# Attention's row maxima from the high parts alone: two heads as a pair of matmuls on the upper and lower 64 rows of TensorE's array

## The chip, the cores and the metric

The kernel runs on one core of a Trainium2 chip. A core has a matrix engine (TensorE, in the profile PE for its matmuls and PEld for its weight loads), three engines for everything else (VectorE is DVE, ScalarE is ACT, GpSimd is POOL), and SyncE (SP), which here issues most of the DMA transfers. The metric is the time of one execution on the device, in microseconds (us); lower is better.

## The reference

One layer of an encoder: RMSNorm, one input projection, grouped-query attention beside a Hyena operator (long convolutions through Fourier transforms), an output projection, an MLP, a last RMSNorm. The change touches the attention, of 2048 positions, 8 query heads and 2 key/value heads of 64 elements:

```python
def one_block(q_blk):
    s = jnp.einsum('bqkgd,bskd->bkgqs', q_blk, k, preferred_element_type=jnp.float32) * scale
    p = jax.nn.softmax(s, axis=-1).astype(v.dtype)
    return jnp.einsum('bkgqs,bskd->bqkgd', p, v)

o = lax.map(one_block, qb)          # blocks of 128 queries
```

The softmax subtracts a bound from the scores of each query before the exponential. Any number near the row's maximum does, since it cancels in the quotient; the kernel works out such a bound from the scores themselves.

## The kernel before, in words

**Precision.** Where float32 accuracy is wanted, a number is split into a high part that TensorE's fast format (`F32R`) holds exactly, and the low rest. `mm3` makes one product of three matmuls of such parts (its lines L158, L159, L160 are shared by the whole kernel). In the attention, a query column of 128 rows in `q` holds the 64 high parts of a head in its upper half (rows 0 to 63) and the 64 low parts in its lower half. A key tile `kt` comes in two versions: the first repeats the high parts of the keys in both halves of the rows, so one matmul of 128 rows gives (high + low of q) times (high of k).

**Units.** `attention` goes through 32 units: a unit is one block of 128 queries (`NT` = 16 blocks) for the four heads (`G`) that share a key/value head (`NKV` = 2). Each unit is 16 steps of `peak` and 16 steps of `weights`, and `peak` runs `AHEAD` = 22 steps earlier.

- `peak(u, i)`: for one head and one of four blocks of 512 keys, one 128x128 by 128x512 matmul into a PSUM bank `sc` (L454), and one VectorE reduction to the maximum of each query (`top`, L457). There are three `sc` banks; the tiles `sh` and `of` take theirs from the same three. After step 15, VectorE forms `low` and `diag` of the 16 maxima of a query.
- `shift`: one matmul (`sh`, L467) turns the maxima into the lower rows of `q2`, so that the score matmul subtracts them.
- `weights(u, j)`: for one block of 128 keys and all four heads, two matmuls into a bank `st` (L474, L475), ScalarE's exponential into `p` (L477, `PB` buffers), and GpSimd's running sum (L482).
- `weighted`: eight steps' products `p` times the values (`o`, L495), in plain float32. Even and odd key blocks use a weight tile of 64 columns each, in the left and the right half of the array's columns (the profile writes 128*64); their outputs are the upper and lower halves of one bank.
- `finish`: four small matmuls (`of`, L506), the division, and the store.

**Side work.** Each step also pumps one piece of other work, `side`: the taps of the long filter (`ft`, L1200) and the projection `uo` (`u_proj`, through `mm3`), whose weights VectorE splits (`uw`, L356).

**Order.** In this part of the program the order of each engine's instructions is set by a scheduler, which starts from the order of the calls above and moves instructions by what is ready. The parts that come later are written down in a fixed order. `load_q` is called by `begin` one unit ahead; `q` and `q2` have three buffers each, and their loads stand in SP's queue.

Of the kernel before, what the change touches and what calls it, by code (L numbers as in the profile page):

```python
# [12 lines left out]
F32R = mybir.dt.float32r  # L13
I32 = mybir.dt.int32
AF = mybir.ActivationFunctionType
ALU = mybir.AluOpType
AX = mybir.AxisListType
# [3 lines left out]
P = 128  # L21
# [4 lines left out]
HD = 64  # L26
NQ = 8
NKV = 2
G = NQ // NKV
# [8 lines left out]
def f32(ap):  # L38
    return ap.bitcast(F32)
# [126 lines left out]
def qkv_proj(k, pa, ps, side):  # L166
# [126 lines left out]
    for i in range(-1 - XL, NT + FL):  # L293
        if i == 13:
            k.first = load_q(k, 0), {(0, b): load_k(k, k.early, 0, b, 4) for b in range(2)}, load_v(k, k.early, 0)
        if 1 < i + XL + 2 < NT:
            xt[i + XL + 2] = load_x(i + XL + 2)
        e = i - FL
        ending = 0 <= e < NT
        if ending:  # L300
            finish(e, *hl[e], 0)
        if 1 < i < NT:
            oq[i] = project(*aT[i], 0, QW)
        if ending:
            finish(e, *hl[e], 1)
        if 0 <= i + 1 < NT:
            aT[i + 1] = turned(i + 1, xs.pop(i + 1))
        if 0 <= i + XL + 1 < NT:
            xs[i + XL + 1] = normed(i + XL + 1, xt.pop(i + XL + 1))
        if 0 <= i + 1 < 2:  # L310
            oq[i + 1] = project(*aT[i + 1], 0, QW)
        pump(side, 1 if i > 0 else 0)
        if ending:
            finish(e, *hl.pop(e), 2)
        if 0 <= i < NT:
            okv = project(*aT.pop(i), QW, 256)
        if 0 <= i - 1 < NT:
            hl[i - 1] = twice(norm_rope(i - 1, *yz.pop(i - 1)))
        if 0 <= i < NT:
            yz[i] = taken(i, oq.pop(i), okv)  # L320
# [89 lines left out]
def load_k(k, pool, kv, b, bufs):  # L410

    c = []
    for part in range(2):
        t = pool.tile([P, 512], F32R, name="kt", bufs=bufs)
        k.nc.sync.dma_start(out=f32(t[:]), in_=k.k_d[kv, part, :, b * 512:(b + 1) * 512])
        c.append(t)
    return c


def load_q(k, n):  # L420

    kv, t = n // NT, n % NT
    q = k.early.tile([P, G, P], F32R, name="q", bufs=3)
    q2 = k.early.tile([P, G, P], F32R, name="q2", bufs=3)
    src = k.q_d[kv * G:(kv + 1) * G, :, t * P:(t + 1) * P].rearrange("h p t -> p h t")
    k.nc.sync.dma_start(out=f32(q[:]), in_=src)
    k.nc.sync.dma_start(out=f32(q2[:HD]), in_=src[:HD])
    return q, q2


def load_v(k, pool, half):
    v = pool.tile([P, NT // 2, NKV, HD], F32, name="vt", bufs=1)
    t0 = half * NT // 2
    k.nc.sync.dma_start(out=v[:], in_=k.v_d[t0:t0 + NT // 2].rearrange("t p h e -> p t h e"))
    return v


def attention(k, a1, ps, side):


    nc = k.nc
# [7 lines left out]
    nc.vector.tensor_copy(out=ones[:], in_=one[:])  # L449

    def peak(u, i):
        b, h = i // G, i % G
        s = ps.get("sc", "sc")
        nc.tensor.matmul(s[:], u.q[:, h], kt[u.kv, b][0][:], start=True, stop=True)  # L454
        if i == 0:
            u.top = a1.tile([P, G, 4], F32, name="top", bufs=2)
        nc.vector.tensor_reduce(out=u.top[:, h, b:b + 1], in_=s[:], axis=AX.X, op=ALU.max, negate=True)  # L457
        if i == 15:
            low = a1.tile([P, G], F32, name="low", bufs=2)
            nc.vector.tensor_reduce(out=low[:], in_=u.top[:], axis=AX.X, op=ALU.min)  # L460
            u.diag = a1.tile([P, G, P], F32R, name="diag", bufs=2)
            nc.vector.tensor_mul(out=u.diag[:], in0=k.ident[:].unsqueeze(1).to_broadcast([P, G, P]),
                                 in1=low[:].unsqueeze(2).to_broadcast([P, G, P]))
# [6 lines left out]
    def weights(u, j):  # L470
# [4 lines left out]
        nc.tensor.matmul(s[:], hi[:, c], u.q[:].rearrange("p h t -> p (h t)"), start=False, stop=True)  # L475
        p = a1.tile([P, 512], F32, name="p", bufs=PB)
        nc.scalar.activation(out=p[:], in_=s[:], func=AF.Exp)  # L477
# [36 lines left out]
    def begin(n):  # L514
        u = Ctx()
        u.kv, u.t = n // NT, n % NT
        u.q, u.q2 = qs.pop(n)
        if n + 1 < NKV * NT:
            qs[n + 1] = load_q(k, n + 1)
        if n == 0:  # L520
            vt.append(load_v(k, a1, 1))
        if 0 < n < NT and n % 3 == 0 and n // 3 <= 3:
            kt[1, n // 3 - 1] = load_k(k, a1, 1, n // 3 - 1, 10)
        return u

    qs, kt, vt = {0: k.first[0]}, k.first[1], [k.first[2]]
# [7 lines left out]
    for step in range(-AHEAD, total + FIN + 1):  # L534
        if 0 <= step < total:
            hold.append(weights(units[step // 16], step % 16))
        if step == 16 * NT - 12:
            kt[1, 3] = load_k(k, k.early, 1, 3, 4)
        i = step + AHEAD
        if i < total:  # L540
            if i % 16 == 0:
                units.append(begin(i // 16))
            peak(units[i // 16], i % 16)
        if i >= SH + 16 and (i - SH) % 16 == 0 and i - SH <= total:
            shift(units[(i - SH) // 16 - 1])
        due += RATE
        pump(side, int(due))
        due -= int(due)
        if len(hold) >= RUN + LAG or step >= total and hold:
            for x in hold[:RUN]:  # L550
                weighted(*x)
            if hold[RUN - 1][1] == 15:
                done, end = hold[0][0], step + FIN
            del hold[:RUN]
        if done and step >= end:
            finish(done)
            done = None
# [5 lines left out]
LAG, RUN = 2, 8  # L563
AHEAD = 22
SH = 2
PB = 14
RATE = 1.0
MA, MB = 1, 6
START = 0
# [1169 lines left out]
```

## Time and profile before

| | |
|---|---|
| runs, median (lowest to highest) | 3235.96 us (3233.48 to 3236.99) |
| the profiled execution | 3238.18 us, span of the trace 3236.1 us |
| PE busy over the span | 3018.8 us (93%) |
| attention, from its first `sc` to its last `o` | about 228 to 1213 us |
| the 512 `sc` matmuls (L454) | mean 409 ns, busy 207.2 us |
| the 512 reductions `top` (L457) | mean 685 ns, busy 346.8 us |
| the 1024 `o` records (L495) | mean 599 ns, busy 234.9 us |

How to read it: matmuls are pipelined, so a record of 400 ns overlaps the next one, which starts some 230 ns later; busy time counts the overlap once, and what one matmul costs TensorE is the distance between starts. Each plain float32 matmul of `o` leaves two records. "Idle before" is the time that an engine stood still just before a group's instructions, with the instruction that released it.

### The profile page before, as it was taken

What the parts mean: (1) busy time and instruction counts of PE and PEld (TensorE: products, weight loads), DVE (VectorE), ACT (ScalarE), POOL (GpSimd) and SP (SyncE); (2) the same over time, 40 slices, a digit from 0 to 9 for tenths busy, and PEclk for the clock granted to TensorE, in tenths of its full rate; (3) what the DMA queues carried; (4) which work ended last, traced back from release to release, by engine and by line L of the source; (5) the groups of instructions that cost most, each with busy time, mean ns of one, the idle gap of its engine ahead of it and who ended that gap; (6) DMA issues with size and microseconds to landing.
All of it is one profiled execution on the core that took longest, in us unless ns stands there. A gap on an engine that the chain in (4) does not pass through costs nothing.

```text
span 3236.1 us, 41557 instructions
## 1 busy us (share of the span) xinstructions
PE 3018.8 (93%) x13732; PEld 2300.6 (71%) x13732; DVE 2190.4 (68%) x3394; ACT 1523.1 (47%) x2774; POOL 1811.1 (56%) x1403
## 2 busy tenths in 40 slices
PE   8978999999999998897979888999999989999998
PEld 6755666666666667665757677888788878888887
DVE  7988776666665547889787667677977635454455
ACT  7866565555554445675555454333433223223333
POOL 3434777778777885658675115776776636241010
PEclk9988999999999999998999889999999999999999
DMA  7757334335225227875745456444644385333464
GB/s 225 226 155 218 124 110 159 104 110 166 100 104 170 91 87 227 258 246 174 223 143 174 166 163 192 152 147 150 215 159 150 121 286 206 126 120 130 134 184 156
DMA packets 494722, 530.00 MB, mean 164 GB/s; under 512 B 40228, under 2 KB 361252, under 8 KB 487468
## 3 DMA queue, kind: packets, MB, share of 16 engines
q1 hardware_dynamic: 489596, 523.38, 50.7%
q10 hardware_dynamic: 4912, 3.97, 0.5%
q8 instruction: 109, 1.79, 0.2%
q14 instruction: 105, 0.86, 0.1%
HBM read 327.76 MB, written 199.50 MB: 163 GB/s over the span
## 4 chain that ended last, share of the span: by engine, by line
PE 42%; POOL 3%; DVE 3%; issue 2%; DMA 2%; ACT 1%; SPq 0%; POOLq 0%; ACTq 0%; DVEq 0%
PE y L159 6%; PE y L158 6%; PE y L160 6%; PE g L160 5%; PE g L159 5%; PE g L158 5%; PE op L158 1%; PE op L159 1%; PE op L160 1%; PE bt L1562 1%; PE cs L1479 1%; PE mt L738 1%; POOL F L1494 0%; PE yo L159 0%; PE yo L158 0%
## 5 line engine op out<-in xcount | busy, mean ns | idle before, releaser
L482 POOL TENSOR_TENSOR sum<-sum,p 128x512 f32<-128x512 f32 x416 | 552.9, 1329 | 132.3 <-ACT p L477 106.6
L457 DVE TENSOR_REDUCE top<-sc 128x1 f32<-128x512 f32 x512 | 346.8, 685 | 257.5 <-PE sc L454 254.7
L477 ACT ACTIVATE p<-st 128x512 f32<-128x512 f32 x512 | 303.3, 597 | 310.4 <-PE st L475 296.6
L158 PE MATMUL g<-mh,wop 128*128 128x512 f32 x896 | 356.0, 397 | 6.8 <-ACT wop L813 6.8
L159 PE MATMUL g<-ml,wop 128*128 128x512 f32 x896 | 355.9, 397 | 3.6 <-DVE ml L824 3.6
L160 PE MATMUL g<-mh,wop 128*128 128x512 f32 x896 | 355.6, 397 | 0.4 <-DVE wop L814 0.4
L990 DVE TENSOR_TENSOR ah<-ar,ah 128x1024 fp32r<-128x1024 f32 x111 | 152.0, 1370 | 231.5 <-ACT ah L989 231.4
L158 PE MATMUL y<-bh,ah 128*128 128x512 f32 x768 | 300.3, 391 | 8.2 <-ACT bh L981 8.2
L159 PE MATMUL y<-bh,ah 128*128 128x512 f32 x768 | 300.4, 391 | 0.8 <-DVE bh L982 0.8
L160 PE MATMUL y<-bh,ah 128*128 128x512 f32 x768 | 300.0, 391 | 0.0
L989 ACT CAST ah<-ar 128x1024 fp32r<-128x1024 f32 x111 | 117.0, 1054 | 347.2 <-PE y L160 337.3
L495 PE MATMUL o<-p,vt 128*64 128x512 f32 x1024 | 234.9, 599 | 0.0
L454 PE MATMUL sc<-kt,q 128*128 128x512 f32 x512 | 207.2, 409 | 12.9 <-DVE top L457 10.8
L474 PE MATMUL st<-q,kt 128*128 128x512 f32 x512 | 214.9, 420 | 1.3 <-ACT p L477 1.3
L475 PE MATMUL st<-q,kt 128*128 128x512 f32 x512 | 203.6, 398 | 0.0
L158 PEld LDWEIGHTS g<-mh,wop 128*128 128x128 f32 x896 | 169.4, 189 | 47.6 <-ACT wop L813 7.0
L159 PEld LDWEIGHTS g<-ml,wop 128*128 128x128 f32 x896 | 169.3, 189 | 45.4 <-DVE ml L824 4.9
L160 PEld LDWEIGHTS g<-mh,wop 128*128 128x128 f32 x896 | 169.2, 189 | 41.7 <-DVE wop L814 1.1
L813 ACT CAST wop<-ws 128x512 fp32r<-128x512 f32 x128 | 79.1, 621 | 228.8 <-PE g L160 203.1
L158 PEld LDWEIGHTS y<-bh,ah 128*128 128x128 f32 x768 | 144.9, 189 | 39.6 <-ACT bh L981 9.0
L159 PEld LDWEIGHTS y<-bh,ah 128*128 128x128 f32 x768 | 144.8, 189 | 31.2 <-DVE bh L982 1.4
L160 PEld LDWEIGHTS y<-bh,ah 128*128 128x128 f32 x768 | 145.0, 189 | 30.2
(322 smaller groups left out, 7621.8 us busy)
## 6 DMA issues: line engine op xcount, KB each, us to landing
ar<-H_d SPq DMA_DIRECT2D x111, 512.0 KB, 3.9
uw<-uw_d SPq DMA_DIRECT2D x36, 1024.0 KB, 4.9
w1raw<-in_w_mlp_in SPq DMA_DIRECT2D x64, 512.0 KB, 4.2
H_d<-r SPq DMA_DIRECT2D x96, 256.0 KB, 2.3
H_d<-s SPq DMA_DIRECT2D x96, 256.0 KB, 2.0
F_d<-F SPq DMA_DIRECT2D x34, 512.0 KB, 3.3
F<-F_d SPq DMA_DIRECT2D x34, 512.0 KB, 4.1
aT<-aT_d SPq DMA_DIRECT2D x32, 512.0 KB, 6.1
```

Source lines behind the costliest of these rows:

```text
L158: mm(out, l_hi, r_hi, start=start, stop=False)
L159: mm(out, l_hi, r_lo, start=False, stop=False)
L160: mm(out, l_lo, r_hi, start=False, stop=stop)
L454: nc.tensor.matmul(s[:], u.q[:, h], kt[u.kv, b][0][:], start=True, stop=True)
L457: nc.vector.tensor_reduce(out=u.top[:, h, b:b + 1], in_=s[:], axis=AX.X, op=ALU.max, negate=True)
L474: nc.tensor.matmul(s[:], lo[:, c], u.q2[:].rearrange("p h t -> p (h t)"), start=True, stop=False)
L475: nc.tensor.matmul(s[:], hi[:, c], u.q[:].rearrange("p h t -> p (h t)"), start=False, stop=True)
L477: nc.scalar.activation(out=p[:], in_=s[:], func=AF.Exp)
L482: nc.gpsimd.tensor_add(out=u.sum[:], in0=u.p0[:] if j == 1 else u.sum[:], in1=p[:])
L495: nc.tensor.matmul(u.o[cols], vt[j // 8][:, j % 8, u.kv], p[:], start=j < 2, stop=j > 13)
L989: nc.scalar.copy(out=h[:, 0], in_=raw[:])
L990: nc.vector.tensor_sub(out=h[:, 1], in0=raw[:], in1=f32(h[:, 0]))
```

## The change

`peak` makes the maxima from the high parts alone: 64 rows instead of 128. Heads 2n and 2n+1 form a pair. `load_q` loads a third tile `q3`, with the high parts of the even heads in rows 0 to 63 and of the odd heads in rows 64 to 127 (two transfers of 64 partitions). At every even step `peak` issues both heads' matmuls, one from the upper 64 rows of `q3` and `kt`, the other from the lower 64, each into a bank of its own, then both reductions; at the odd steps it issues nothing. The numbers of matmuls (512), of weight loads and of reductions stay as they were. In the built program the pair's tile is 64 rows by 128 columns, at rows 0 and 64. To make room for `q3`, `PB` goes from 14 to 13. The score matmuls of `weights` keep high and low parts.

```diff
 def load_q(k, n):
     kv, t = n // NT, n % NT
     q = k.early.tile([P, G, P], F32R, name="q", bufs=3)
     q2 = k.early.tile([P, G, P], F32R, name="q2", bufs=3)
     src = k.q_d[kv * G:(kv + 1) * G, :, t * P:(t + 1) * P].rearrange("h p t -> p h t")
     k.nc.sync.dma_start(out=f32(q[:]), in_=src)
     k.nc.sync.dma_start(out=f32(q2[:HD]), in_=src[:HD])
-    return q, q2
+    q3 = k.early.tile([P, G // 2, P], F32R, name="q3", bufs=3)
+    for i in range(2):
+        k.nc.sync.dma_start(out=f32(q3[i * HD:(i + 1) * HD]), in_=src[:HD, i::2])
+    return q, q2, q3
...
     def peak(u, i):
-        b, h = i // G, i % G
-        s = ps.get("sc", "sc")
-        nc.tensor.matmul(s[:], u.q[:, h], kt[u.kv, b][0][:], start=True, stop=True)
+        b, pair = i // G, i % G // 2
         if i == 0:
             u.top = a1.tile([P, G, 4], F32, name="top", bufs=2)
-        nc.vector.tensor_reduce(out=u.top[:, h, b:b + 1], in_=s[:], axis=AX.X, op=ALU.max, negate=True)
+        if i % 2 == 0:
+            s = [ps.get("sc", "sc") for _ in range(2)]
+            for r in range(2):
+                rows = slice(r * HD, (r + 1) * HD)
+                nc.tensor.matmul(s[r][:], u.q3[rows, pair], kt[u.kv, b][0][rows], start=True, stop=True)
+            for r in range(2):
+                h = 2 * pair + r
+                nc.vector.tensor_reduce(out=u.top[:, h, b:b + 1], in_=s[r][:], axis=AX.X, op=ALU.max, negate=True)
...
-        u.q, u.q2 = qs.pop(n)
+        u.q, u.q2, u.q3 = qs.pop(n)
...
-PB = 14
+PB = 13
```

The lines move by ten: L454 becomes L464, L474 and L475 become L484 and L485, L495 becomes L505.

TensorE's queue in the middle of the attention, before: the rows from one group of `o` on. `x8` is eight in a row, and the shapes are those of the outputs.

```order
L495 MATMUL o<-p,vt 64x512 x8
L474 MATMUL st<-q_8905,kt 128x512
L475 MATMUL st<-q,kt 128x512
L454 MATMUL sc<-kt,q 128x512
L158 MATMUL uo<-aT,uw 128x512
L159 MATMUL uo<-aT,uw 128x512
L160 MATMUL uo<-aT,uw 128x512
L474 MATMUL st<-q_8905,kt 128x512
L475 MATMUL st<-q,kt 128x512
L454 MATMUL sc<-kt,q 128x512
```

The same place after the change (`q_9803` is the tile `q3`, `q_9493` the tile `q2`):

```order
L505 MATMUL o<-p,vt 64x512 x8
L484 MATMUL st<-q_9493,kt 128x512
L485 MATMUL st<-q,kt 128x512
L464 MATMUL sc<-kt,q_9803 128x512 x2
L484 MATMUL st<-q_9493,kt 128x512
L485 MATMUL st<-q,kt 128x512
L158 MATMUL uo<-aT,uw 128x512
L159 MATMUL uo<-aT,uw 128x512
L160 MATMUL uo<-aT,uw 128x512
L484 MATMUL st<-q_9493,kt 128x512
L485 MATMUL st<-q,kt 128x512
L464 MATMUL sc<-kt,q_9803 128x512 x2
```

The `sc` matmuls now stand two together, after every second pair of `st`, each time between matmuls of the whole array. Over the program, 246 of the 256 pairs stand next to each other (240 alone, six in two runs of three), and in ten, nine of them among the first, other matmuls come between the two halves. None stands next to a group of `o`.

SP's queue a little earlier in the attention, before, with the loads of one unit's queries:

```order
L362 DMA uw_d<-uw 128x2048
L350 DMA uraw<-in_w_in 128x8x128
L1207 DMA taps_d<-taps 128x512
L427 DMA q_4628<-q_d 64x4x128
L426 DMA q<-q_d 128x4x128
L407 DMA u_d<-uy 128x511
L362 DMA uw_d<-uw 128x2048
L1207 DMA taps_d<-taps 128x512
```

After:

```order
L1217 DMA taps_d<-taps 128x512
L431 DMA q_4940<-q_d 64x2x128 x2
L407 DMA u_d<-uy 128x511
L1201 DMA tr<-in_trow 128x512
L362 DMA uw_d<-uw 128x2048
L350 DMA uraw<-in_w_in 128x8x128
L1217 DMA taps_d<-taps 128x512
L428 DMA q_4652<-q_d 64x4x128
L427 DMA q<-q_d 128x4x128
```

Each unit's loads gain the two of `q3` (L431, each of half the partitions and two heads), which stand some way ahead of those of `q2` and `q` (L428, L427).

## The prediction

> **What bounds the kernel now.** I read the page first, for the engines and the costliest groups. The lines of it that matter, for each group its count, then busy time, mean of one, and idle time before it with what ended it:
>
> ```profile
> span 3236.1 us, 41557 instructions
> PE 3018.8 (93%) x13732; PEld 2300.6 (71%) x13732; DVE 2190.4 (68%) x3394; ACT 1523.1 (47%) x2774; POOL 1811.1 (56%) x1403
> ...
> L482 POOL TENSOR_TENSOR sum<-sum,p 128x512 f32<-128x512 f32 x416 | 552.9, 1329 | 132.3 <-ACT p L477 106.6
> L457 DVE TENSOR_REDUCE top<-sc 128x1 f32<-128x512 f32 x512 | 346.8, 685 | 257.5 <-PE sc L454 254.7
> ...
> L454 PE MATMUL sc<-kt,q 128*128 128x512 f32 x512 | 207.2, 409 | 12.9 <-DVE top L457 10.8
> ```
>
> VectorE's reductions wait 254.7 us for the `sc` matmuls, and those wait 10.8 us for VectorE. An average over the span doesn't say what holds the attention, so next the table by stretches: its opening (228 to 270), the whole stage, and one stretch in its middle. The columns are the length, then busy time and count for PE, PEld, DVE, ACT and POOL, the granted clock, the DMA share and GB/s.
>
> ```profile
> 228.00:270.00 42.00, 22.36 (x49) 12.37 (x50) 24.82 (x58) 20.00 (x44) 0.00 (x0) 0.58 0.93 213
> 228.00:1213.00 985.00, 944.45 (x4068) 622.80 (x4069) 631.89 (x1019) 522.20 (x995) 726.82 (x551) 0.97 0.42 130
> ...
> 600.00:700.00 100.00, 100.00 (x447) 66.73 (x446) 63.78 (x98) 55.11 (x101) 77.87 (x60) 1.00 0.33 110
> ```
>
> From 270 us on TensorE is the bound: in the middle it is busy all the time at full clock, and POOL, the next, is at 78 of 100. In the opening it stands still half the time, so what is saved or lost there counts little. Then the waits of TensorE in the stage (us in total, times, longest):
>
> ```profile
> PE sc L454 <- DVE top L457: 10.8, 3, 4.4
> ...
> PE sh L467 <- DVE top L457: 8.3, 3, 3.4
> PE of L506 <- DVE top L457: 5.2, 3, 2.6
> ```
>
> Those three, 24.3 us, are all that VectorE's reductions cost it. So a change of TensorE's work in the attention reaches the end one for one, up to a gain of 258 us (985 less POOL's 727).
>
> Since busy time hides drains, the price of this change must come from distances between starts. The timeline around one group of `o`, the one place where the kernel already leaves the whole array for tiles of it:
>
> ```profile
> 520.14 0.40 PE L160 MATMUL uo<-aT,uw 128*128 128x512 f32 x1
> 520.47 0.20 PEld L495 LDWEIGHTS o<-p,vt 128*64 128x64 f32 x4 [0.36 <-issue]
> 520.47 3.65 PE L495 MATMUL o<-p,vt 128*64 128x512 f32 x16
> 520.95 0.14 PEld L495 LDWEIGHTS o<-p,vt 128*64 128x64 f32 x2 [0.28 <-issue]
> 521.38 0.14 PEld L495 LDWEIGHTS o<-p,vt 128*64 128x64 f32 x2 [0.29 <-issue]
> ...
> 523.10 0.14 PEld L495 LDWEIGHTS o<-p,vt 128*64 128x64 f32 x2 [0.28 <-issue]
> 524.05 0.19 PEld L474 LDWEIGHTS st<-q,kt 128*128 128x128 f32 x1 [0.81 <-issue]
> 524.05 0.50 PE L474 MATMUL st<-q,kt 128*128 128x512 f32 x1
> 524.16 0.19 PEld L475 LDWEIGHTS st<-q,kt 128*128 128x128 f32 x1
> ...
> 524.39 0.40 PE L475 MATMUL st<-q,kt 128*128 128x512 f32 x1
> 524.39 0.19 PEld L454 LDWEIGHTS sc<-kt,q 128*128 128x128 f32 x1
> 524.63 0.40 PE L454 MATMUL sc<-kt,q 128*128 128x512 f32 x1
> ...
> 524.86 0.40 PE L158 MATMUL uo<-aT,uw 128*128 128x512 f32 x1
> ```
>
> The length of one `o` record (minimum, median, maximum in ns) is in the answer on that tile:
>
> ```profile
> L495 PE MATMUL o<-p,vt x1024: 592/592/644, 280.9 to 1211.5; 128*64 128x512 f32 x171
> ```
>
> Four things are to be seen. *The steady pace*: 524.39, 524.63, 524.86, so 0.23 us a matmul, and each one's weights load while the matmul ahead runs. *Halves do run side by side*: 16 records take 3.65 us, two new weight loads every 0.43 us; one after the other, 16 records at 0.43 would take 6.9. *Entering costs*: from 520.14 the next start would be 520.37; it is 520.47 (+0.10), and its weights load only then, not ahead, so the first pass takes 0.48 instead of 0.43 (+0.05 for a load of 64 columns). *Leaving costs*: the last of the eight pairs starts at 520.47 + 3.65 - 0.59 = 523.53, would make room at 523.96 (0.43 later), and the next matmul starts at 524.05 (+0.09); its weights load only then too, and its successor follows after 0.34 instead of 0.23 (+0.11 for 128 columns). One visit to a tiled array costs 0.35 us over the matmuls themselves. That this is the tile and not the change of number format, `of` shows, plain float32 on the whole array between fast-format matmuls:
>
> ```profile
> 526.72 0.40 PE L454 MATMUL sc<-kt,q 128*128 128x512 f32 x1
> 526.96 1.00 PE L506 MATMUL of<-fold,ob 128*128 128x65 f32 x8
> ```
>
> It follows after 0.24, with nothing added.
>
> **The change part by part.** *The pair.* Before, two `sc` matmuls cost 2 x 0.23 = 0.46 us. Now they run as tiles of 64 rows, alone between matmuls of the whole array. I take the pair's own time as one matmul, 0.23, since the two halves of `o` overlap wholly. Added: entering 0.10, the load of 128 columns 0.11 (the size that the load at 524.05 has, not the 0.05 of 64 columns), leaving 0.09, the next load 0.11, together 0.41. So 0.64 for 0.46: +0.18 us a pair. The bounds of this unknown price: nothing at all for the switches, a pair at 0.24 (the distance 526.72 to 526.96), hence -0.22; or all of it and the two halves one after the other, 0.64 + 0.23 = 0.87, hence +0.41. I take +0.18, since the `o` rows are the nearest, the same array and a tile of half of it, though of columns and not of rows.
>
> The Trainium skill, page "TensorEngine Tiling (Array Packing)", section Tiling Modes, speaks against the change in the same sense: a change of the tiling mode, not of the tile alone, drains the engine, rows or columns alike. The rows at 520.47 and 524.05 agree for columns; for rows no run here shows it yet.
>
> *How many.* The stretches again, for the line of `sc` alone (PE busy and count, PEld, clock):
>
> ```profile
> 228.00:270.00 42.00, 12.50 (x21) 5.96 (x21) 0.58 0.93 213
> 270.00:1213.00 943.00, 194.66 (x491) 93.06 (x491) 0.99 0.39 126
> ```
>
> 21 matmuls lie in the opening, where 42 us hold 22 us of matmuls and TensorE waits anyhow: I count nothing there. The other 491 are 245 pairs. Of the ten pairs that the new order separates nine are among the first; each would pay two visits and overlap nothing, 0.82 us, so 8 us if none is hidden. I take 240 pairs and nothing for the separated ones: 240 x 0.18 = +43 us.
>
> *The banks and VectorE.* The count and length of the reductions stay (512 x 0.69). A pair takes two of three banks at once, so the second matmul comes a step earlier than it did and VectorE's lead shrinks. Where VectorE is behind is seen at one of the long runs of weight splits:
>
> ```profile
> 505.81 4.59 DVE L356 SCALAR_TENSOR_TENSOR uw<-uraw,g,uw 128x128 fp32r<-128x128 f32 x5
> 510.32 0.68 DVE L457 TENSOR_REDUCE top<-sc 128x1 f32<-128x512 f32 x1
> ```
>
> Bounds: the 24.3 us of such waits go, because TensorE is slower and VectorE as fast (-24), or double (+24). I take zero, between the two: both reasons are real and the rows favour neither.
>
> *The loads.* 64 more transfers in SP's queue, ahead of those of `q2` and `q`. The nearest are L427's:
>
> ```profile
> L427 SPq DMA_DIRECT2D q<-q_d x32: 585/586/683, 68.9 to 1125.8; - x32
> ...
> DMA to landing us min/median/max: 2.9/4.5/5.6
> ```
>
> Two issues of 0.59 us a unit, in a unit of 943/32 = 29 us, and landing after 5.6 at worst, a unit ahead of use: the lead of some 20 us hides them, 0 taken. If SP were so blocked that each unit waited one landing, it would be 32 x 5.6 = 179; nothing in TensorE's waits names a query load, so I leave that out. *`PB` 13*: ten `p` tiles are held by the order of the calls, so three are spare instead of four; ScalarE's waits for GpSimd are
>
> ```profile
> ACT p L477 <- POOL sum L482: 7.4, 11, 0.8
> ```
>
> and end in no wait of TensorE that names them. 0 taken, +7 at most if they double and reach it.
>
> *Sum.* The profiled execution is 3238.2, its span 3236.1 and 2.1 around it; 3238.2 + 43 = 3281. The profiled one stands 2.2 above the median of the runs, so the forecast against the median is 3279.
>
> **The rivals.** *A, the forecast*: the switches are paid in full and the halves overlap; 3279, and with VectorE's term and the size of the entry load (0.05 instead of 0.11: 240 x 0.06 = 14 less) from 3250 to 3310.
>
> *B, the other side: the array changes to rows without a drain, and the weights load ahead.* For it: halves of rows leave the columns as they are, unlike the tiles of `o`, so the rows above need not hold; the loads are 0.19 us long against matmuls 0.23 apart. Against it: both loads at a switch of `o` start only after the switch. A pair would cost 0.24: 240 x -0.22 = -53, 3183. The point from which it decides is a visit dearer than 0.23 us: below it the change gains.
>
> The Trainium skill, page "TensorE: Matmul & The Clock Gate", Part 3 (the mechanism), has such a rule: weights for other row groups load during running matmuls, and each further tile adds about 4 ns to a pack's span. By it the pair would cost 0.23 and the whole come to B's time; the rows of `o` bear out the overlap and not the loading ahead.
>
> *C, the halves don't overlap*: two tiles of 64 rows write all 128 partitions of two banks, which the halves of `o` never did. Then +0.41 a pair: 240 x 0.41 = +98, 3334.
>
> *D, half of the price*: only the drains are paid (0.10 + 0.09) and the loads hidden, or the like; between -0.04 and +0.06 a pair, so 3226 to 3250.
>
> **How the numbers follow.** A 0.60, B 0.17, C 0.08, D 0.15. The runs before span 3.5 us, so 0.2% (6.5 us, about what a measurement of this kernel can tell from no change) is the bound of "same". D is faster in 0.04, same in 0.05, slower in 0.06. Faster: 0.17 + 0.04 = 0.21; same 0.05; slower 0.60 + 0.08 + 0.06 = 0.74. The range has A, all of D and the lower half of C, and the edge of B: 3210 to 3335. The likeliest's own is 3250 to 3310.
>
> **What would show it.** In the new timeline: two `sc` starts a few ns apart (C: 0.23 apart); the pair's weight loads starting with the pair, 0.33 after the matmul ahead (B: during it, and 0.23); the next matmul 0.43 after the pair, the one behind it 0.34 later. The stage should last some 1028 us from its first `sc` to its last `o`, with PE's busy time about what it was or lower although the stage is longer, the reductions' mean still 0.69, and every later stage as long as before. I am wrong if the visit is cheaper than 0.23 us, or if VectorE's waits at `sc` grow to tens of us; the list of TensorE's waits would name `top`.

## The result: slower by 0.74 to 0.78%, in the forecast direction and smaller than forecast

The changed kernel takes 3259.84 us (median of 4 runs, 3255.65 to 3265.72) against 3234.72 before; ratio 1.0078, 95% interval 1.0061 to 1.0096. A second series on another occasion gave 3257.63 against 3232.19, ratio 1.0074 (1.0059 to 1.0090). That is some 25 us slower; the forecast was 43. The profiled execution took 3255.65 us.

The page of the changed kernel, its span and the reductions:

```profile
span 3253.6 us, 41673 instructions
...
L467 DVE TENSOR_REDUCE top<-sc 128x1 f32<-128x512 f32 x512 | 329.9, 684 | 301.7 <-PE sc L464 300.8
```

VectorE's reductions are as many and as long (684 ns), and wait longer for the `sc` matmuls (300.8 us, before 254.7): the attention is held by TensorE more than it was. The last records of `o` say how much the stage grew; the two times are the starts of the first and the last, here of the changed kernel:

```profile
L505 PE MATMUL o<-p,vt x1024: 592/592/643, 285.3 to 1232.0; 128*64 128x512 f32 x171
```

Before it was 280.9 to 1211.5. So at the end of the attention the changed kernel is 20.5 us behind; the two profiled spans differ by 17.5, since the later stages, which the change doesn't touch, took 3 us less in this execution.

Now the pair itself, TensorE's timeline in the middle, first the matmuls and then the weight loads:

```profile
601.28 0.40 PE L485 MATMUL st<-q,kt 128*128 128x512 f32 x1
601.61 0.49 PE L464 MATMUL sc<-kt,q 64*128 64x512 f32 x2
602.03 0.50 PE L1210 MATMUL ft<-hc,w4h 128*128 128x512 f32 x1
602.37 0.40 PE L1210 MATMUL ft<-hc,w4l 128*128 128x512 f32 x1
```

```profile
601.06 0.19 PEld L485 LDWEIGHTS st<-q,kt 128*128 128x128 f32 x1
601.61 0.18 PEld L464 LDWEIGHTS sc<-kt,q 64*128 64x128 f32 x2 [0.36 <-issue]
602.03 0.19 PEld L1210 LDWEIGHTS ft<-hc,w4h 128*128 128x128 f32 x1 [0.24 <-issue]
602.14 0.19 PEld L1210 LDWEIGHTS ft<-hc,w4l 128*128 128x128 f32 x1
```

The two halves and both their loads fit in one record's length (0.49 and 0.18 us): they run side by side. But the pair starts 0.33 us after the matmul ahead, not 0.23; the next one 0.42 later; the one behind it after 0.34. From 601.28 to 602.37 that is 1.09 us for what took 4 x 0.23 = 0.92 before. And each load stands at the start of its own matmul, where the load at 601.06 runs ahead of its.

What the pair costs the stage is best read where TensorE waits for nobody. The table by stretches (length, PE, PEld, DVE, ACT, POOL, clock, DMA, GB/s), before:

```profile
270.00:600.00 330.00, 313.76 (x1345) 206.50 (x1344) 244.52 (x400) 193.25 (x398) 240.36 (x182) 0.98 0.46 143
600.00:900.00 300.00, 299.92 (x1328) 199.52 (x1327) 188.57 (x288) 164.02 (x301) 235.21 (x179) 1.00 0.37 119
```

after:

```profile
270.00:600.00 330.00, 327.60 (x1353) 184.09 (x1352) 227.84 (x400) 195.56 (x398) 244.31 (x184) 0.99 0.46 147
600.00:900.00 300.00, 299.85 (x1269) 170.70 (x1268) 182.55 (x280) 158.28 (x288) 226.18 (x171) 1.00 0.38 121
```

From 600 to 900 TensorE is busy throughout in both, and gets 1269 matmuls done instead of 1328. From 270 to 600 it gets *more* done than before, 1353 instead of 1345, though every pair costs more. That is where most of the rest of the forecast 43 us went: before, TensorE stood still or ran slowly there for some of the time, and now it hardly does.

### The profile page after: what moved, and what is told of

It reads as the page before. It is cut to its first block, busy times and chain, and to the rows that moved or that the text cites. A ratio compares the mean times of both kernels' runs of the same rounds, so it can differ in the third digit from the quotient of the medians.

```text
span 3253.6 us, 41673 instructions
## 1 busy us (share of the span) xinstructions
PE 3053.3 (94%) x13732; PEld 2227.8 (68%) x13732; DVE 2166.9 (67%) x3394; ACT 1527.0 (47%) x2774; POOL 1814.4 (56%) x1403
## 4 chain that ended last, share of the span: by engine, by line
PE 41%; POOL 4%; DVE 3%; issue 2%; DMA 1%; ACT 1%; SPq 0%; POOLq 0%; DVEq 0%; ACTq 0%
PE y L159 6%; PE y L160 6%; PE y L158 6%; PE g L160 5%; PE g L159 5%; PE g L158 5%; PE cs L1489 1%; PE bt L1572 1%; PE op L158 1%; PE op L159 1%; PE op L160 1%; POOL F L1504 1%; DMA h<-h_d 1%; POOL F L1505 1%; PE yo L159 0%
## 5 line engine op out<-in xcount | busy, mean ns | idle before, releaser
L467 DVE TENSOR_REDUCE top<-sc 128x1 f32<-128x512 f32 x512 | 329.9, 684 | 301.7 <-PE sc L464 300.8
L505 PE MATMUL o<-p,vt 128*64 128x512 f32 x1024 | 233.8, 598 | 0.0
L484 PE MATMUL st<-q,kt 128*128 128x512 f32 x512 | 217.0, 424 | 0.0
L485 PE MATMUL st<-q,kt 128*128 128x512 f32 x512 | 204.0, 398 | 0.0
L158 PE MATMUL uo<-aT,uw 128*128 128x512 f32 x384 | 168.2, 438 | 0.3 <-DMA uw<-uw_d 0.2
```

The source lines that it names most:

```text
L158: mm(out, l_hi, r_hi, start=start, stop=False)
L467: nc.vector.tensor_reduce(out=u.top[:, h, b:b + 1], in_=s[r][:], axis=AX.X, op=ALU.max, negate=True)
L484: nc.tensor.matmul(s[:], lo[:, c], u.q2[:].rearrange("p h t -> p (h t)"), start=True, stop=False)
L505: nc.tensor.matmul(u.o[cols], vt[j // 8][:, j % 8, u.kv], p[:], start=j < 2, stop=j > 13)
```

## Experiments

The theory after the result: (1) every visit to the tiled array costs about 0.39 us beyond its matmuls, 39 us in all, and (2) some 15 to 20 us of waits on VectorE went, because TensorE became slower and VectorE did not. Rivals: the new order of the pairs, not the slower TensorE, took the waits away; the loads of `q3` or `PB` 13 cost something; the price is in the two halves together and not in the visit.

**The order of the pairs without the tiles.** Both heads' matmuls stand together as in the change, with all 128 rows of `q`; there is no `q3`, and `PB` is 14. Against the change, in `peak`:

```diff
-                rows = slice(r * HD, (r + 1) * HD)
-                nc.tensor.matmul(s[r][:], u.q3[rows, pair], kt[u.kv, b][0][rows], start=True, stop=True)
+                nc.tensor.matmul(s[r][:], u.q[:, 2 * pair + r], kt[u.kv, b][0][:], start=True, stop=True)
```

> The kernel before, with the maxima issued two heads at a time as in the change, but each head a matmul of all 128 rows (no q3, PB 14): the order and the banks of the change without the tiles. Theory 1 (the price is the visit to the tiled array; the waits on VectorE went because TensorE became slower): no visits, the pair costs 0.46 us as before, the waits of TensorE on VectorE stay at some 20 to 30 us; time within 8 us of before (3227 to 3243). Theory 2 (the waits went because of the new order of the pairs): the 16 us of waits go without any visit, 3219 or so, faster than both.

Measured: 3234.79 us against 3232.19, ratio 1.0008 (0.9998 to 1.0018), the same as before. TensorE's waits on `top` in this run's attention, first with the opening, then from 270 us on:

```profile
PE sc L458 <- DVE top L461: 27.0, 11, 5.3
```

```profile
PE sc L458 <- DVE top L461: 15.8, 8, 4.1
```

The 27.0 us are what they were before, in other places (24.3 for `sc`, `sh` and `of` together). Of those 24.3, the 10.8 at `sc` lie in the opening, so from 270 us on it is 15.8 against 13.5. The order takes no waits away, and issuing two heads at once, with two banks at once, costs nothing that shows. With the next run, which holds the loads, the change's loss is left to the tiles.

**The loads and `PB` alone.** The kernel before with `load_q` of the change, `q3` unused, and `PB` 13.

```diff
+    q3 = k.early.tile([P, G // 2, P], F32R, name="q3", bufs=3)
+    for i in range(2):
+        k.nc.sync.dma_start(out=f32(q3[i * HD:(i + 1) * HD]), in_=src[:HD, i::2])
...
-PB = 14
+PB = 13
```

> The kernel before with the loads of q3 and PB 13, q3 unused: what the change adds beside the matmuls. Theory 1: nothing, 3235 within 5 us, since the loads are a unit ahead and three p tiles are spare. Rival: the SP queue or the p tiles cost some of the difference of 25 us, 3240 to 3260.

Measured: 3235.61 us, ratio 1.0006 (0.9995 to 1.0017). Neither costs anything that shows.

**One matmul a visit.** Each head's 64-row matmul at its own step, even heads on the upper half and odd ones on the lower. Against the change:

```diff
-        b, pair = i // G, i % G // 2
+        b, h = i // G, i % G
+        pair, r = h // 2, h % 2
+        rows = slice(r * HD, (r + 1) * HD)
+        s = ps.get("sc", "sc")
+        nc.tensor.matmul(s[:], u.q3[rows, pair], kt[u.kv, b][0][rows], start=True, stop=True)
...
-        if i % 2 == 0:
-            s = [ps.get("sc", "sc") for _ in range(2)]
...
```

> The change, but each head's 64-row matmul issued at its own step, as in the kernel before: some 490 visits of one matmul each instead of 245 visits of two. Theory 1 (each visit costs about 0.39 us beyond the matmuls themselves, whether it holds one or two): a lone matmul costs 0.62 us instead of 0.23, +0.39 x 490 = +191 us over before, less the waits on VectorE that go (up to 25): 3235 + 170 to 190 = 3405 to 3425. Rival (the price is in using two halves together, such as two banks written at once): a lone one costs little, about 3235 to 3260.

Measured: 3391.73 us, ratio 1.0482 (1.0461 to 1.0502), 159.5 us over before. A lone matmul in its timeline:

```profile
700.04 0.40 PE L482 MATMUL st<-q,kt 128*128 128x512 f32 x1
...
700.36 0.50 PE L461 MATMUL sc<-kt,q 64*128 64x512 f32 x1
...
700.79 0.50 PE L158 MATMUL uo<-aT,uw 128*128 128x512 f32 x1
...
701.13 0.40 PE L159 MATMUL uo<-aT,uw 128*128 128x512 f32 x1
```

0.32, 0.43 and 0.34 us, as for a pair: the visit costs the same 0.40 us over three times 0.23 with one matmul in it as with two. The price is in the visit, and the second half is free. The total lies 13 us below the expected range. The trace has 484 visits from 270 us on, some 190 us at this price, and no wait on `top` is left there; TensorE's idle time there is 19.6 us less than before, and the slow stretches behind waits, which are worked out further below, take off another 5 us. That leaves some 165 us, against the 159.5 measured.

**Two pairs a visit.** All four heads of a key block at every fourth step; that needs four `sc` banks, so `u` has one.

```diff
-        if i % 2 == 0:
-            s = [ps.get("sc", "sc") for _ in range(2)]
-            for r in range(2):
+        if i % 4 == 0:
+            s = [ps.get("sc", "sc") for _ in range(4)]
+            for h in range(4):
+                pair, r = h // 2, h % 2
                 rows = slice(r * HD, (r + 1) * HD)
...
-                with Banks(k, "ps2", {"st": 2, "sc": 3, "o": 1, "u": 2}) as ps:
+                with Banks(k, "ps2", {"st": 2, "sc": 4, "o": 1, "u": 1}) as ps:
```

> The change with all four heads of a key block in one visit, every fourth step: two pairs in a row, which takes four sc banks, so u has one bank instead of two. Theory 1: half as many visits, each 0.39 + 2 x 0.23 = 0.85 us for four matmuls that cost 0.93 before, -0.07 x 123 = -9 us against the kernel before, if the one bank of u costs nothing (its own run tells that), so 3223, less what waits on VectorE add. Rival (the price grows with the tiled matmuls, not with the visits): 3255 or so as the change.

Its control is the kernel before with these banks:

> The kernel before with four sc banks and one u bank: the control for the run with two pairs a visit. Theory 1: a fourth bank gives VectorE more room, some of the 24 us of waits go, -5 to -15; one bank of u makes the next group of uo wait for ScalarE's copy of 0.59 us, 48 groups, up to +28. Between 3220 and 3255; no theory of the visits hangs on it alone.

Measured: 3244.06 us with two pairs a visit (ratio to before 1.0044, 1.0030 to 1.0058), 3238.15 for the control (1.0022, 1.0011 to 1.0033). The visit is what was expected:

```profile
702.45 0.40 PE L485 MATMUL st<-q,kt 128*128 128x512 f32 x1
...
702.77 0.73 PE L465 MATMUL sc<-kt,q 64*128 64x512 f32 x4
...
703.44 0.50 PE L158 MATMUL uo<-aT,uw 128*128 128x512 f32 x1
...
703.77 0.40 PE L159 MATMUL uo<-aT,uw 128*128 128x512 f32 x1
```

1.32 us from 702.45 to 703.77, for what costs 6 x 0.23 = 1.38 on the whole array: the first arrangement in which the tiles gain, by 0.06 us for four matmuls, some 7 us for 123 visits. The forecast of 3223 was missed all the same. The banks alone cost some 6 us (3238.15 against 3232.56 before in this series), and this kernel stays 6 us above its control instead of 7 below it. The rival, 3255 as the change, is wrong too: half as many visits are 14 us better than the change.

The traces show where the gain went. From 270 us on, only 108 visits have all four matmuls; the scheduler split the rest into 32 smaller ones (four of three matmuls, 16 of two, 12 of one). And the `o` matmuls stand in 97 groups, with other work between them, where the control has 83 and the kernel before 65. An estimate from the prices read here: 108 gains of 0.06 are -6.5 us; 20 visits of two or three at +0.17 (one of three takes 1.32 us as well) and 12 of one at +0.40 are +8.2; 14 more groups of `o` at the prediction's 0.35 are +4.9. The sum is +6.6, and 5.9 was measured.

**Shorter reductions.** Before and after, each with the reduction over 256 of the 512 scores, which leaves out half of the maxima.

```diff
-        nc.vector.tensor_reduce(out=u.top[:, h, b:b + 1], in_=s[:], axis=AX.X, op=ALU.max, negate=True)
+        nc.vector.tensor_reduce(out=u.top[:, h, b:b + 1], in_=s[:, :256], axis=AX.X, op=ALU.max, negate=True)
```

In the change it is `s[r][:]` that becomes `s[r][:, :256]`.

> The kernel before, with each reduction over the first 256 of the 512 scores only (half of the maxima left out): VectorE is relieved of some 512 x 0.3 = 150 us, TensorE's work is the same. Theory 1 (the waits on VectorE, 24 us in the list for top and up to 20 more for taps and of, are TensorE's only loss here): 15 to 30 us faster, 3203 to 3218. Rival (the waits come from GpSimd or from the order): no change, 3232.

> The change with the same halved reductions. Theory 1: here most of the waits are gone already, so it gains less, 5 to 15 us, 3242 to 3253; against the kernel before with halved reductions it is slower by the bare price of the visits, 245 x 0.16 = 39 us or so (the pair's distances 0.33 + 0.42 + 0.34 against 4 x 0.23, less a matmul). Rival: the difference between the two stays 25 us.

Measured: before 3223.78 us (ratio 0.9972, 0.9959 to 0.9985), the change 3255.24 (1.0074, 1.0060 to 1.0088, to the kernel before). The first gains 9 us, less than the 15 to 30 expected. The second gains nothing that can be told from none, where 5 to 15 were expected: its ratio to the kernel before is the 1.0074 of the change itself. The direction fits point (2) of the theory, VectorE's time is worth more before than after. But the halved reductions, 0.42 us instead of 0.69, take little from the waits on `top` between 270 and 600 us: 9.3 us are left of 13.5. So most of those waits come from what stands ahead of the reductions.

**Half of the weight splits on GpSimd.** In the first third, VectorE splits the weights `uw` in runs of splits of 0.73 us in the mean, and the reductions queue behind them. `UW_VEC` names those that VectorE does.

```diff
-UW_VEC = 0, 1, 2, 3, 4, 5, 6, 7
+UW_VEC = 0, 2, 4, 6
```

> The kernel before, with half of the weight splits uw (four of eight in each group, 48 in all) moved from VectorE to GpSimd, two instructions each there. Theory 1 (TensorE's waits in the first half of the attention come from reductions that queue behind the runs of splits on VectorE): the runs of 0.7 us splits are halved, most of the waits on top (24 us in the trace before) go; GpSimd takes some 48 x 0.8 = 38 us in a stretch where it is busy for 72 of 100: 3215 to 3228, faster than both kernels. Rival (GpSimd then holds the p tiles): 3232 to 3250.

> The change with half of the splits on GpSimd. Theory 1: little is left to be won, since the slower TensorE has already given VectorE its time: 0 to 8 us off 3258, 3250 to 3258, and 30 to 40 us slower than the kernel before with the same splits. Rival (the waits are as large as before): 15 us off, 3243.

Measured: the kernel before with these splits 3224.13 us (ratio 0.9979, 0.9968 to 0.9990), faster than both kernels by a little; the change with them 3262.64 (1.0094, 1.0079 to 1.0110). TensorE's waits from 270 to 600 us, in the kernel before, and then with half of the splits on GpSimd:

```profile
PE sh L467 <- DVE top L457: 8.3, 3, 3.4
PE of L506 <- DVE top L457: 5.2, 3, 2.6
...
PE sc L454 <- DVE u L383: 1.3, 1, 1.3
PE st L474 <- ACT p L477: 1.3, 1, 1.3
```

```profile
PE of L506 <- POOL ob L500: 8.9, 4, 3.4
PE sh L467 <- DVE top L457: 1.2, 1, 1.2
PE st L474 <- ACT p L477: 0.4, 1, 0.4
```

The waits on `top` fall from 13.5 to 1.2 us, and 8.9 us on GpSimd's `ob` come in their place: the engine that took the splits is late next. In the changed kernel nothing was to be gained; it got 3 to 5 us slower, where 0 to 8 faster was expected.

Both with half of the splits on GpSimd, the change is 38.5 us slower than the kernel before, close to the bare price of the visits, 39. That is chance, as the first and last `o` of the two traces show, the kernel before ahead of the change:

```profile
L495 PE MATMUL o<-p,vt x1024: 592/592/644, 278.8 to 1203.1; 128*64 128x512 f32 x171
```

```profile
L505 PE MATMUL o<-p,vt x1024: 592/592/1117, 295.2 to 1240.8; 128*64 128x512 f32 x171
```

Of the 37.7 us at the last `o`, 16.4 have arisen before the first, in the opening, and only 21.3 behind it, where the visits are. There, from 270 us on, the kernel before still waits 14.4 us on `ob`, and the change 4.0.

**A quarter of them.** `UW_VEC = 0, 1, 2, 4, 5, 6`.

> The same with two of eight splits on GpSimd (24 in all). Theory 1: part of the gain, 3220 to 3230. Rival: no change, 3232.

Measured: 3232.43 us, ratio 1.0003 (0.9993 to 1.0012): nothing, where theory 1 had expected part of the gain. Runs of three splits leave the reductions late enough: the waits on `top` between 270 and 600 us are 12.1 us, against 13.5. So that these waits come from the runs of splits is borne out by the half and not by a steady course.

**The change again.**

> The changed kernel once more, for its time beside these runs on the same chip and a second trace. Both theories: 3255 to 3266, the distances between starts at a pair 0.33, 0.42 and 0.34 us again.

Measured: 3257.63 us. In its trace the distances at a pair are the same, and the `o` matmuls stand later than in the first trace (285.3 to 1232.0):

```profile
L505 PE MATMUL o<-p,vt x1024: 592/592/644, 290.4 to 1235.8; 128*64 128x512 f32 x171
```

So the two executions differ by 5 us in the opening, and not behind it. In the second, TensorE ran at half of the clock until 284 us, in the first until 275.

## Why the prediction was right, and what it mis-sized

**The pair: right, step by step.** Forecast: entering 0.10, a load of 128 columns 0.11, leaving 0.09, the next load 0.11, the two halves as one matmul; a pair at +0.18 us. Measured from the rows: 0.33, 0.42 and 0.34, together 1.09 instead of 0.92, +0.17 with the page's two decimals. Over many pairs it is a little less: `diag`, once a unit, tells the length of a unit between 600 and 900 us (ten starts; the first and the last), before

```profile
L462 DVE TENSOR_TENSOR diag<-ident,low x10: 678/1046/1762, 620.8 to 879.6; 128x512 fp32r<-128x512 f32 x10
```

and after

```profile
L472 DVE TENSOR_TENSOR diag<-ident,low x10: 678/1406/1764, 618.5 to 888.9; 128x512 fp32r<-128x512 f32 x10
```

(879.6 - 620.8) / 9 = 28.76 us and (888.9 - 618.5) / 9 = 30.04: +1.29 a unit, 0.16 for each of eight pairs. So 245 x 0.16 = 39 us for all pairs instead of the 43. The rows of `o`, tiles of half of the columns, foretold tiles of half of the rows within a few hundredths of a us. By the rule of the Trainium skill, page "TensorEngine Tiling (Array Packing)", section Tiling Modes, that a change of mode drains the engine, the trace now agrees for rows as well (0.33 into it, 0.42 out of it). Rivals B (3183) and C (3334) are out: the loads at 601.61 and 602.03 are not ahead, and the halves overlap. D, with at most +0.06 a pair and 3250 us, is out by the +0.16. Of the rule on tiles in the Trainium skill, page "TensorE: Matmul & The Clock Gate", Part 3, the side-by-side half holds here (0.49 us for two, one record's length). That weights load ahead does not show here: around a pair, where the tiling mode changes, they start with their own matmul.

**The loads and `PB`: right**, nothing, as the run with them alone shows.

**The banks and VectorE: the step that was mis-sized.** It was bounded by -24 and +24, and zero was taken between them, because "the rows favour neither". Some 21 us came back, near the lower bound, though not as the bound was worked out. Of its 24.3 us, the 10.8 at `sc` lie in the opening, where the changed kernel waits as long (11.3). From 270 to 600 us TensorE's whole list in the changed kernel is

```profile
PE sc L464 <- DVE top L467: 2.0, 3, 1.0
```

where the one before held 16.1 us, 13.5 of them on `top`. Over the rest of the stage, the length less PE's busy time gives TensorE's idle time, before (to the last `o`) and after:

```profile
270.00:1211.50 941.50, 920.59 (x4015) 609.60 (x4015) 607.07 (x962) 501.44 (x949) 725.38 (x550) 0.99 0.39 126
```

```profile
270.00:1232.00 962.00, 957.03 (x4013) 544.77 (x4012) 579.73 (x959) 504.56 (x947) 728.46 (x550) 0.99 0.40 127
```

That is 20.9 us against 5.0, so 15.9 us less, 11.5 of them on `top`. And some waits cost more than their length, as the trace of before shows behind one of them:

```profile
507.70 0.40 PE L454 MATMUL sc<-kt,q 128*128 128x512 f32 x1
511.06 0.77 PE L467 MATMUL sh<-diag,ones 128*128 128x512 f32 x1 [2.96 <-DVE top L457]
511.63 0.63 PE L158 MATMUL uo<-aT,uw 128*128 128x512 f32 x1
512.05 0.63 PE L159 MATMUL uo<-aT,uw 128*128 128x512 f32 x1
...
514.58 0.40 PE L159 MATMUL uo<-aT,uw 128*128 128x512 f32 x1
```

After 2.96 us of standing still the matmuls are some 0.42 us apart instead of 0.23 until 514.6, seven of them: 1.3 us more. Not every wait is followed so. Five waits on `top` in the trace of before last some 2 us or more, and the clock (third figure from the end) behind them, in order of time, is

```profile
352.50:355.90 3.40, 3.40 (x15) 2.78 (x16) 2.52 (x6) 2.23 (x5) 0.18 (x1) 1.00 1.04 308
371.20:374.60 3.40, 3.40 (x10) 2.63 (x9) 1.62 (x6) 1.48 (x3) 1.31 (x2) 0.50 0.83 290
416.20:419.60 3.40, 3.40 (x15) 2.78 (x16) 2.44 (x7) 1.49 (x3) 1.44 (x2) 1.00 0.51 193
463.40:466.80 3.40, 3.40 (x10) 2.63 (x9) 1.51 (x5) 2.10 (x5) 1.28 (x1) 0.51 0.88 268
511.20:514.50 3.30, 3.30 (x8) 2.62 (x9) 1.61 (x6) 1.02 (x2) 0.00 (x0) 0.50 0.67 278
```

Three of the five are followed by 3.4 us at half of the clock, which costs some 5 us in all (half of 3 x 3.4). In the changed kernel no such stretch stands between 275 and 600 us. So 15.9 + 5 = 21 us came back, in these two traces.

That TensorE's slower pace, and not the new order, took the waits away, is shown by two runs. With the order alone, 15.8 us on `top` remain from 270 us on. With single visits, the order before and TensorE slower still, the whole list from 270 us on is

```profile
PE of L513 <- POOL ob L507: 1.3, 1, 1.3
```

The reason was written down in the prediction (TensorE is slower and VectorE as fast), and the tie with "the second matmul comes a step earlier" was wrong: the order alone cost nothing that can be told from no change (3234.79 against 3232.19).

**The opening: a small miss.** The ten separated pairs were taken at nothing. The first `o` starts 4.4 us later than before (285.3 to 280.9). The run with the order alone shows that the tiles are the cause. From the first `sh` to the first `o` both kernels do the same 47 matmuls, 12 of them `sc` that stand alone; first the order alone, then the change:

```profile
265.71 0.79 PE L471 MATMUL sh<-diag,ones 128*128 128x512 f32 x1
...
280.87 3.65 PE L499 MATMUL o<-p,vt 128*64 128x512 f32 x16
```

```profile
265.06 0.80 PE L477 MATMUL sh<-diag,ones 128*128 128x512 f32 x1
...
285.35 3.65 PE L505 MATMUL o<-p,vt 128*64 128x512 f32 x16
```

The change takes 20.3 us for them instead of 15.2. Twelve lone visits at 0.40 make 4.8 of the 5.1. The clock has a part in it too: it is at half until 275 us in the change, and until 272 with the order alone. In the two traces of the change, in that of single visits and in that of the change with half of the splits on GpSimd, the clock stays at half until 275 to 296 us and the first `o` comes at 285 to 295 us; why it stays so longer with tiles is open.

**The sum as it came out.** 39 for the pairs, 4.4 for the opening, less 21 that came back, is 22; the stage grew by 20.5. The forecast is right by its main term, the pair. That it came out 18 us too high is mostly the waits, which were taken at zero; the miss at the opening hid a part of that.

## What to carry to other kernels

A few small matmuls as tiles of the array are dear when the array is the bound and each stands alone between matmuls of the whole: the way in and out costs nearly two matmuls (0.40 us against 0.23 each), so a pair loses, two pairs in a row win a little at the visit (0.06 us, which this kernel lost again elsewhere). Longer runs should pay by this reckoning; none was tried. Look for a place where the kernel already changes over, and take the distance between starts there, since busy time shows none of it. And when the bounding engine is made slower or faster by a term, ask what the engines behind it do with the time: about half of the loss came back here as waits that went. Whether a change that saves as much would lose it again in the same way, no run here shows.

## What the runs showed of the hardware

A tile of 64 rows needs as long for its weights as the whole array (0.18 against 0.19 us), and two such loads run at once. Weights for a tile of 64 rows, and those for the matmul of the whole array behind it, load only with their own matmul (601.61 and 602.03), where others load ahead. With both switches a visit costs 0.40 us over three steady paces, with one matmul in it as with two.

A wait of TensorE can be followed by 3.4 us at half of the clock (0.42 instead of 0.23 us a matmul), and the length of the wait alone doesn't decide it. Here three of five waits of some 2 us or more on `top` were followed so, and the longest of the five, 3.4 us, was not; in the run of single visits one of 1.3 us was:

```profile
1113.80:1117.10 3.30, 3.30 (x8) 1.77 (x6) 3.30 (x5) 0.60 (x1) 3.12 (x3) 0.50 0.38 151
```
